# A hybrid decoder layer on one core: attention values computed with channels on partitions

## The chip, the cores and the metric

The kernel runs on one core of one Trainium2 chip. A core has TensorE (PE in the profile: matrix products and transposes, results into PSUM), VectorE (DVE), ScalarE (ACT), GpSimd (POOL) and a queue (SP) that issues the loads and stores. Each engine works through its own list in order; the engines meet through semaphores. The metric is device time in microseconds; lower is better.

## The reference, cut to what matters

One layer normalises `x` (256 rows, 1024 channels), projects it to 3840 columns, runs three branches on pieces of the projection, gates each branch with a SiLU, joins them and projects back. The change touches the attention branch (8 heads of 64 channels) and the normalisation inside the convolution branch:

```
l_own = where(dist >= 0, q @ k.T * scale - slopes * dist, NEG)   # per head, 256 x 256
p     = softmax(l_own, axis=-1)
y_m   = merge_heads(p @ v) * silu(m_gate)
...
yn    = (conv - mean) * rsqrt(var + eps) * ln_g + ln_b           # over the 256 conv channels
y_a   = (silu(yn) @ pw_w + pw_b) * silu(a_gate)
```

With 256 rows there is one attention block, so no block selection takes place.

## The kernel before, in words

Every large product is done in split form: each weight and each activation is held as a high part and a low remainder (`hi`/`lo` for weights, `xh`/`xl` for the input), and three products of a special 32-bit type are added. ACT makes the high part (line 113), DVE or POOL the low one (line 119). Products of plain float32 (scores, values, transposes) run beside them.

The projection is cut into steps, `STEPS`, in a fixed order. A step of kind `slot` makes 128 output channels with channels on partitions: 16 products with `hi`, then whatever is planned for the step's middle, then 8 with `lo`. A step of kind `row` makes a quarter of a sum over input channels for 512 output channels, with sequence rows on partitions: 8 products of 512 columns, the middle, 4 more. The tables `mid` and `then` (lines 481 to 513) say which piece of the branches stands in the middle of a step and which behind it. The order is thus written by hand: steps `mv0` to `mv3` (values), `mg0` to `mg3` (attention gate), then `mq0, mk0, mq1, mk1, ...` for four pairs of heads, then the output projection in passes `o0` to `o3` (each with a middle) and the rest of it.

For each pair of heads `hp`: `scores` multiplies queries and keys into two PSUM banks `p_sc`, one head each; DVE adds the bias and takes the extreme (442), ACT takes the exponential into `pr` and its sum into `sm` (444). `turn` transposes `pr` on PE into `p_pt` and copies it out to `pt` (454). `values` multiplies `pt` with `mv` into `p_o` with rows on partitions (465, 467); DVE divides by the sum (469) and multiplies by the gate (471). `back` transposes that to channels on partitions (476), and `put_y` splits it for the output projection (302, 303).

The convolution's taps run on DVE as a chain of 62 operations (328), spread over the steps by `FILL`. `conv_norm` transposes the result and takes its statistics; `conv_back` scales it (351), transposes it back (355) and applies the SiLU; `conv_point` is the small matrix product after that.

PSUM gives eight banks: six in a rotating pool (`bank`) and two at the side. A tile that takes over a bank waits until the last reader of the earlier one is done.

Of the kernel before, what the change touches and what calls it, by code (L numbers as in the profile page):

```python
# [35 lines left out]
A_VAL, A_GLU, A_GATE, R_Q, R_K, R_V, R_GATE, M_Q, M_K, M_V, M_GATE = (  # L36
    0, 256, 512, 768, 1024, 1280, 1536, 1792, 2304, 2816, 3328)
# [2 lines left out]

STEPS = ["rq0", "rk0", "rq1", "rk1", "ag0", "ag1"] + [f"mv{i}" for i in range(4)] + \
    [f"mg{i}" for i in range(4)] + ["mq0", "pw"] + [f"{a}{i}" for i in range(4) for a in ("mq", "mk")][1:]
SLOT = {"rq": R_Q, "rk": R_K, "ag": A_GATE, "mq": M_Q, "mk": M_K}
ROW = {"mv": M_V, "mg": M_GATE}
CH = 32

FILL = {"rq0": 4, "rk0": 5, "rq1": 4, "rk1": 4, "ag0": 4, "ag1": 5, "mv0": 5, "mv1": 5, "mv2": 5, "mv3": 5, "mg0": 5,
# [4 lines left out]
def hybrid(ctx: ExitStack, tc: tile.TileContext, xt, xn, wi, wo, taps, pw, fg, dec, bias, out):  # L52
    nc = tc.nc
    const = ctx.enter_context(tc.tile_pool(name="const", bufs=1))
    rawp = ctx.enter_context(tc.tile_pool(name="rawp", bufs=RAW))
    hlp = ctx.enter_context(tc.tile_pool(name="hlp", bufs=PARTS))
    work = ctx.enter_context(tc.tile_pool(name="work", bufs=2))
# [5 lines left out]
    def bank(name):  # L63
        return psum.tile([P, 512], F32, name=name, tag="ps")
# [10 lines left out]
    tiny = const.tile([P, 2], F32, name="tiny")  # L75
# [4 lines left out]
    ident = const.tile([P, P], F32, name="ident")  # L80
# [105 lines left out]
    rstd = const.tile([P, 2], F32, name="rstd")  # L186
# [63 lines left out]
    nc.scalar.copy(out=rb_sb, in_=rb[:, :SEQ])  # L250

    mv = const.tile([P, 2, 512], F32, name="mv")
    mg = const.tile([P, 2, 512], F32, name="mg")
    rv = const.tile([P, 2, 256], F32, name="rv")
    rgate = const.tile([P, 2, 256], F32, name="rgate")

# [37 lines left out]
    def scaled(dst, p):  # L294
        nc.vector.tensor_tensor(out=dst, in0=p, in1=rb_sb, op=ALU.mult)
# [50 lines left out]

    norms = []

    def conv_back():
        for b, p, mvv, rs in norms:  # L350
            nc.vector.tensor_scalar(yn[:, b], p[:, :256], mvv[:, 0:1], rs, op0=ALU.subtract, op1=ALU.mult)
        for c in range(2):
            p = bank(f"p_z{c}")[:, :SEQ]
            for b in range(2):
                nc.tensor.transpose(p[:, b * P:(b + 1) * P], yn[:, b, c * P:(c + 1) * P], ident)
            nc.scalar.activation(sh[:, c], p, AF.Silu, bias=lnb[c], scale=lng[c])
            nc.scalar.activation(p, p, AF.Silu, bias=lnb[c], scale=lng[c])
            nc.vector.tensor_tensor(out=sll[:, c], in0=p, in1=sh[:, c].bitcast(F32), op=ALU.subtract)
# [12 lines left out]
    rq, rk, st = {}, {}, {}  # L371

    def heads(p, name):

        t = work.tile([P, SEQ], F32, name=name, tag=name)
        scaled(t, p)
        return t
# [47 lines left out]
            put_y(2 + c, p)  # L425


    mq, mk, pt, pr, sms, po = {}, {}, {}, {}, {}, {}

    def scores(hp):  # L430
        ps = [bank(f"p_sc{hp}{a}") for a in range(2)]
        for lhs, n, o in ((slice(P, 256), 256, 0), (slice(0, P), P, 256)):
            for a in range(2):
                r = slice(HD * a, HD * (a + 1))
                nc.tensor.matmul(ps[a][:, o:o + n], mq[hp][r, lhs], mk[hp][r, :n], start=True, stop=True)  # L435
        sms[hp] = work.tile([P, 2, 2], F32, name="sm", tag="sm")
        for a in range(2):
            h = 2 * hp + a
            pr[h] = work.tile([P, 384], F32, name="pr", tag="st", bufs=4)
            mn = work.tile([P, 2], F32, name="mn", tag="mn", bufs=4)  # L440
            for b, s in ((1, slice(0, 256)), (0, slice(256, 384))):
                nc.vector.tensor_tensor_reduce(ps[a][:, s], ps[a][:, s], bias_sb[h // 4][:, h % 4, s], -0.125, 3.0e38,  # L442
                                               ALU.add, ALU.min, mn[:, b:b + 1])
                nc.scalar.activation(pr[h][:, s], ps[a][:, s], AF.Exp, bias=mn[:, b:b + 1], scale=-1.0,  # L444
                                     accum_out=sms[hp][:, b, a:a + 1])

    def turn(hp):
        for a in range(2):
            h = 2 * hp + a
            p = bank(f"p_pt{h}")  # L450
            for o, s in ((0, 256), (P, 0), (256, P)):
                nc.tensor.transpose(p[:, o:o + P], pr[h][:, s:s + P], ident)
            pt[h] = work.tile([P, 384], F32, name="pt", tag="pt", bufs=3)
            (nc.scalar.copy if a else nc.vector.tensor_copy)(out=pt[h], in_=p[:, :384])
        ri = work.tile([P, 2, 2], F32, name="ri", tag="ri")
        nc.vector.reciprocal(ri, sms[hp])
        sms[hp] = ri

    def values(hp):
        p = bank(f"p_o{hp}")[:, :SEQ].rearrange("p (b c) -> p b c", c=P)  # L460
        for b in range(2):
            for a in range(2):
                h = 2 * hp + a
                hs, d = slice(h * HD, (h + 1) * HD), slice(a * HD, (a + 1) * HD)
                nc.tensor.matmul(p[:, b, d], pt[h][:, b * P:(b + 1) * P], mv[:, 0, hs], start=True, stop=(b == 0))  # L465
                if b:
                    nc.tensor.matmul(p[:, b, d], pt[h][:, 256:], mv[:, 1, hs], start=False, stop=True)
        p4 = p.rearrange("p b (a d) -> p b a d", d=HD)
        nc.vector.tensor_tensor(out=p4, in0=p4, in1=sms[hp][:, :, :, None].to_broadcast([P, 2, 2, HD]), op=ALU.mult)
        po[hp] = work.tile([P, 2, P], F32, name="po", tag="po")  # L470
        nc.vector.tensor_tensor(out=po[hp], in0=p, in1=mg[:, :, hp * P:(hp + 1) * P], op=ALU.mult)

    def back(hp):
        p = bank(f"p_y{hp}")[:, :SEQ]
        for b in range(2):
            nc.tensor.transpose(p[:, b * P:(b + 1) * P], po[hp][:, b], ident)
        put_y(4 + hp, p)


# [1 line left out]
    first, mid, then = {}, {}, {}  # L481

    def plan(table, name, f, *args):
        table.setdefault(name, []).append(lambda: f(*args))

    def after(name, n):

        order = [s for s in STEPS if s != "pw"] + [f"o{k}" for k in range(4)]
        return order[order.index(name) + n]
# [2 lines left out]
        plan(mid, after(f"rk{c}", 1), ret_scores, c)  # L492
    plan(mid, "mv0", ret_values)
    plan(then, "mv2", ret_back)
    plan(mid, "mg3", conv_norm)
    plan(mid, "mq0", conv_back)
    plan(then, "mq0", lambda: nc.scalar.activation(tiny[:, 1:2], tiny[:, 0:1], AF.Exp))
    plan(mid, "mk1", conv_point)
    for hp in range(4):
        k = f"mk{hp}"  # L500
        plan(mid, after(k, 1), scores, hp)
        late = hp == 3
        plan(mid if late else then, after(k, 3 if late else 2), turn, hp)
# [11 lines left out]
    for name in STEPS:  # L515
        g, i = name[:2], name[-1]
        ahead(at_step[name])
        for f in first.get(name, ()):
            f()
        between = mid.get(name, ())  # L520
        if g == "pw":
            for f in between:
                f()
        elif g in ROW:
            ps = row(name, between)
            if i == "3":
                for b in range(2):
                    if g == "mv":
                        nc.scalar.activation(mv[:, b], ps[b], AF.Copy, scale=rstd[:, b:b + 1])
                    else:  # L530
                        nc.scalar.activation(mg[:, b], ps[b], AF.Silu, scale=rstd[:, b:b + 1])
# [14 lines left out]
    ps = {}  # L546
# [125 lines left out]
```

## Time and profile before

| | |
|---|---|
| median of three runs | 142.26 us (142.19 to 142.7) |
| profiled execution | 143.95 us |
| its span, first to last instruction | 142.2 us |
| mean granted TensorE clock over the span | 0.992 of full speed |
| busy share PE / POOL / DVE / ACT | 94% / 57% / 55% / 50% |
| PE from and to | 0 to 135.2 us |

The profiled execution is 1.75 us longer than its span. A row of a timeline gives start, duration, engine, line, operation, the names read and written and the shape; `x4` means that four instructions of the same kind are merged. A float32 product shows as two records and a special 32-bit one as a single record.

### The profile page before, as it was taken

What the parts mean: (1) busy time and instruction counts of PE and PEld (TensorE: products, weight loads), DVE (VectorE), ACT (ScalarE), POOL (GpSimd) and SP (SyncE); (2) the same over time, 40 slices, a digit from 0 to 9 for tenths busy, and PEclk for the clock granted to TensorE, in tenths of its full rate; (3) what the DMA queues carried; (4) which work ended last, traced back from release to release, by engine and by line L of the source; (5) the groups of instructions that cost most, each with busy time, mean ns of one, the idle gap of its engine ahead of it and who ended that gap; (6) DMA issues with size and microseconds to landing.
All of it is one profiled execution on the core that took longest, in us unless ns stands there. A gap on an engine that the chain in (4) does not pass through costs nothing.

```text
span 142.2 us, 2416 instructions
## 1 busy us (share of the span) xinstructions
PE 133.7 (94%) x884; PEld 118.9 (84%) x884; DVE 77.7 (55%) x212; ACT 71.0 (50%) x128; POOL 81.0 (57%) x51
## 2 busy tenths in 40 slices
PE   7799999999999999999999999999999999999900
PEld 2588899899999998777889999999999888988900
DVE  1446385626897799979936325544353512214460
ACT  4366489927950390059207977518357383102520
POOL 2000002596599998987994589952916639603340
PEclk9999999999999999999999999999999999999996
DMA  4999999499987887066586227667000000000124
GB/s 132 301 354 314 409 406 394 171 378 396 426 295 219 248 312 267 27 191 212 158 272 198 43 113 196 224 202 270 3 0 5 0 0 0 0 5 0 65 82 148
DMA packets 8796, 26.42 MB, mean 186 GB/s; under 512 B 1104, under 2 KB 2384, under 8 KB 8784
## 3 DMA queue, kind: packets, MB, share of 16 engines
q1 hardware_dynamic: 8496, 25.87, 53.2%
q10 hardware_dynamic: 288, 0.39, 0.8%
q8 instruction: 7, 0.11, 0.3%
q14 instruction: 5, 0.04, 0.1%
HBM read 25.21 MB, written 1.05 MB: 185 GB/s over the span
## 4 chain that ended last, share of the span: by engine, by line
PE 87%; DVE 2%; DMA 2%; POOL 2%; ACT 1%; issue 1%; POOLq 0%; DVEq 0%; SPq 0%; ACTq 0%
PE p_a L210 9%; PE p_rv L213 9%; PE p_mv L289 8%; PE p_mg L289 8%; PE p_out L195 4%; PE p_out L197 4%; PE p_out L196 4%; PE p_mq L270 3%; PE p_mk L265 3%; PE p_mk L270 3%; PE p_mq L265 3%; PE p_mq L264 3%; PE p_mk L264 3%; PE p_sc L435 2%; PE p_o L465 2%; DMA raw_g<-in_wi 2%
## 5 line engine op out<-in xcount | busy, mean ns | idle before, releaser
L119 POOL TENSOR_TENSOR lo_o<-raw_o,hi_o 128x1024 fp32r<-128x1024 f32 x8 | 18.9, 2380 | 12.7 <-ACT hi_o L113 8.5
L328 DVE SCALAR_TENSOR_TENSOR sums<-u,tp,sums 128x256 f32<-128x256 f32 x58 | 23.4, 479 | 0.0
L195 PE MATMUL p_out<-hi_o,yh 128*128 128x512 f32 (+1 forms) x40 | 14.5, 362 | 0.0
L196 PE MATMUL p_out<-hi_o,yl 128*128 128x512 f32 (+1 forms) x40 | 13.9, 349 | 0.0
L197 PE MATMUL p_out<-lo_o,yh 128*128 128x512 f32 (+1 forms) x40 | 13.9, 348 | 0.0
L183 POOL TENSOR_TENSOR rstd<-rs_t,mhalf 128x2 f32<-128x2 f32 x1 | 0.7, 720 | 22.4 <-DVE rs_t L182 22.4
L444 ACT ACTIVATE pr<-p_sc,mn 128x256 f32<-128x256 f32 (+1 forms) x16 | 6.7, 421 | 13.3 <-DVE mn L442 13.3
L113 ACT CAST hi_g<-raw_g 128x1024 fp32r<-128x1024 f32 (+1 forms) x10 | 8.8, 876 | 8.7 <-DMA raw_g<-in_wi 8.7
L119 POOL TENSOR_TENSOR lo_mq<-raw_mq,hi_mq 128x1024 fp32r<-128x1024 f32 x4 | 9.6, 2402 | 3.1 <-ACT hi_mq L113 3.1
L119 DVE TENSOR_TENSOR lo_g<-raw_g,hi_g 128x1024 fp32r<-128x1024 f32 (+1 forms) x10 | 10.0, 1006 | 1.3 <-ACT hi_g L113 1.3
L119 POOL TENSOR_TENSOR lo_mk<-raw_mk,hi_mk 128x1024 fp32r<-128x1024 f32 x4 | 9.6, 2406 | 1.0 <-ACT hi_mk L113 1.0
L119 POOL TENSOR_TENSOR lo_mg<-raw_mg,hi_mg 128x1024 fp32r<-128x1024 f32 x4 | 9.5, 2389 | 0.5 <-ACT hi_mg L113 0.5
L442 DVE CUSTOM_DVE_ANT_0 p_sc<-p_sc,bias 128x256 f32<-128x256 f32 (+1 forms) x16 | 5.7, 374 | 7.5 <-ACT pr L444 5.1
L119 POOL TENSOR_TENSOR lo_mv<-raw_mv,hi_mv 128x1024 fp32r<-128x1024 f32 x4 | 9.5, 2390 | 0.0
L197 PEld LDWEIGHTS p_out<-lo_o,yh 128*128 128x128 f32 x40 | 7.5, 188 | 1.1
L176 DVE SCALAR_TENSOR_TENSOR xl<-xt_sb,xh 128x256 fp32r<-128x256 f32 x8 | 3.9, 486 | 8.2 <-ACT xh L175 8.2
L195 PEld LDWEIGHTS p_out<-hi_o,yh 128*128 128x128 f32 x40 | 7.5, 188 | 1.0
L113 ACT CAST hi_o<-raw_o 128x1024 fp32r<-128x1024 f32 x8 | 8.3, 1048 | 0.0
L196 PEld LDWEIGHTS p_out<-hi_o,yl 128*128 128x128 f32 x40 | 7.5, 188 | 0.9
L593 POOL TENSOR_TENSOR yg<-xn_sb,fg_sb 128x512 f32<-128x512 f32 (+1 forms) x3 | 3.3, 1099 | 8.1 <-DVE xn_sb L591 8.1
L264 PE MATMUL p_mq<-xh,hi_mq 128*128 128x256 f32 x32 | 7.8, 284 | 0.0
L265 PE MATMUL p_mq<-xl,hi_mq 128*128 128x256 f32 x32 | 7.7, 279 | 0.0
(175 smaller groups left out, 385.5 us busy)
## 6 DMA issues: line engine op xcount, KB each, us to landing
raw_o<-in_wo SPq DMA_DIRECT2D x8, 512.0 KB, 4.6
raw_g<-in_wi SPq DMA_DIRECT2D x6, 512.0 KB, 7.8
raw_mv<-in_wi SPq DMA_DIRECT2D x4, 512.0 KB, 7.6
raw_mg<-in_wi SPq DMA_DIRECT2D x4, 512.0 KB, 4.9
raw_mq<-in_wi SPq DMA_DIRECT2D x4, 512.0 KB, 4.1
raw_mk<-in_wi SPq DMA_DIRECT2D x4, 512.0 KB, 4.0
bias<-in_bias SPq DMA_DIRECT2D x2, 768.0 KB, 8.5
raw_g<-in_wi SPq DMA_DIRECT2D x4, 256.0 KB, 4.2
```

The source lines that it names most:

```text
L113: nc.scalar.copy(out=hi, in_=raws[j])
L119: eng.tensor_tensor(out=lo, in0=raws.pop(j), in1=hi.bitcast(F32), op=ALU.subtract)
L195: nc.tensor.matmul(p, lh, rh, start=first, stop=False)
L196: nc.tensor.matmul(p, ll, rh, start=False, stop=False)
L197: return nc.tensor.matmul(p, lh, rl, start=False, stop=last)
L210: nc.tensor.matmul(pa[c], wt[:, c * P:(c + 1) * P], xs[:, k], **flags)
L213: nc.tensor.matmul(pv[b], xs[:, k, b * P:(b + 1) * P], wt, **flags)
L264: nc.tensor.matmul(p, hi[:, s], xh[:, k], start=(k == 0), stop=False)
L265: nc.tensor.matmul(p, hi[:, s], xl[:, k], start=False, stop=False)
L270: nc.tensor.matmul(p, lo[:, s], xh[:, k], start=False, stop=(k == KC - 1))
L289: nc.tensor.matmul(row_banks[g][b], (xl if part else xh)[:, k, b * P:(b + 1) * P], (lo if w else hi)[:, s], start=(k == 0 and w == 0 and p ...
L328: nc.vector.scalar_tensor_tensor(to[c], u[:, c, t:t + SEQ], w, sums[c], op0=ALU.mult, op1=ALU.add)
```

## The change

Attention values: `values` now holds `mv` still and streams `pt`, so that `p_o` comes out with channels on partitions: head 0 of the pair on partitions 0 to 63, head 1 on 64 to 127. `back` and its transposes go. Since the row sum can no longer be applied there, `scores` divides by it: the exponential stays in the PSUM bank `p_sc`, and DVE multiplies it by the reciprocal on the way to `pr`. The gate must have channels on partitions too, so `mg0` to `mg3` become four `slot` steps with a DVE scaling and an ACT SiLU each. `turn` and `values` of the first three pairs move half a step or a step later. `conv_norm` moves behind `mg3`, the scaling of `conv_back` becomes `conv_scale` behind `mq0`, and the rest of it stands in the middle of `mk0`.

```diff
-SLOT = {"rq": R_Q, "rk": R_K, "ag": A_GATE, "mq": M_Q, "mk": M_K}
-ROW = {"mv": M_V, "mg": M_GATE}
+SLOT = {"rq": R_Q, "rk": R_K, "ag": A_GATE, "mg": M_GATE, "mq": M_Q, "mk": M_K}
+ROW = {"mv": M_V}
...
-    def conv_back():
+    def conv_scale():
         for b, p, mvv, rs in norms:
             nc.vector.tensor_scalar(yn[:, b], p[:, :256], mvv[:, 0:1], rs, op0=ALU.subtract, op1=ALU.mult)
+
+    def conv_back():
...
-                nc.scalar.activation(pr[h][:, s], ps[a][:, s], AF.Exp, bias=mn[:, b:b + 1], scale=-1.0,
-                                     accum_out=sms[hp][:, b, a:a + 1])
+                nc.scalar.activation(ps[a][:, s], ps[a][:, s], AF.Exp, bias=mn[:, b:b + 1], scale=-1.0,
+                                     accum_out=sm[:, b:b + 1])
+            soft.append((pr[h], ps[a], sm, halves))
+        for p, e, sm, halves in soft:
+            ri = work.tile([P, 2], F32, name="ri", tag="ri", bufs=4)
+            nc.vector.reciprocal(ri, sm)
+            for b, s in halves:
+                nc.vector.tensor_scalar(p[:, s], e[:, s], ri[:, b:b + 1], None, op0=ALU.mult)
...
     def values(hp):
-        p = bank(f"p_o{hp}")[:, :SEQ].rearrange("p (b c) -> p b c", c=P)
-        for b in range(2):
+        p = bank(f"p_o{hp}")[:, :SEQ]
+        for part in range(2):
             for a in range(2):
                 h = 2 * hp + a
-                hs, d = slice(h * HD, (h + 1) * HD), slice(a * HD, (a + 1) * HD)
-                nc.tensor.matmul(p[:, b, d], pt[h][:, b * P:(b + 1) * P], mv[:, 0, hs], start=True, stop=(b == 0))
-                if b:
-                    nc.tensor.matmul(p[:, b, d], pt[h][:, 256:], mv[:, 1, hs], start=False, stop=True)
...
-    def back(hp):
...
+                hs, r = slice(h * HD, (h + 1) * HD), slice(HD * a, HD * (a + 1))
+                if part == 0:
+                    nc.tensor.matmul(p[r], mv[:, 0, hs], pt[h][:, :256], start=True, stop=False)
+                else:
+                    nc.tensor.matmul(p[r, P:], mv[:, 1, hs], pt[h][:, 256:], start=False, stop=True)
+        nc.vector.tensor_tensor(out=p, in0=p, in1=mgate[:, hp], op=ALU.mult)
         put_y(4 + hp, p)
...
-    plan(mid, "mg3", conv_norm)
-    plan(mid, "mq0", conv_back)
-    plan(then, "mq0", lambda: nc.scalar.activation(tiny[:, 1:2], tiny[:, 0:1], AF.Exp))
+    plan(then, "mg3", conv_norm)
+    plan(then, "mq0", conv_scale)
+    plan(mid, "mk0", conv_back)
+    plan(mid, "mk0", lambda: nc.scalar.activation(tiny[:, 1:2], tiny[:, 0:1], AF.Exp))
...
-        late = hp == 3
-        plan(mid if late else then, after(k, 3 if late else 2), turn, hp)
-        plan(mid, after(k, 4 if late else 3), values, hp)
-        if late:
-            plan(then, "o3", back, hp)
-        else:
-            plan(mid, after(k, 4), back, hp)
+        plan(mid, after(k, 3), turn, hp)
+        plan(mid, after(k, 4), values, hp)
...
-            if g == "ag":
-                t = agate[:, int(i)]
+            if g in ("ag", "mg"):
+                t = (agate if g == "ag" else mgate)[:, int(i)]
                 scaled(t, p)
                 nc.scalar.activation(t, t, AF.Silu)
```

PE, before: what stands from behind step `mk1` to the middle of `mk2` beside the projection's own products (`p_pt` are the transposed weights of heads 0 and 1, `p_o` their values, `p_sc` the scores of heads 2 and 3, `p_y` the transposes back).

```order
L452 MATMUL p_pt_1128<-ident,pr 128x128 x3
L452 MATMUL p_pt_1134<-ident,pr 128x128 x3
...
L465 MATMUL p_o_1165<-mv,pt 128x64 x3
L467 MATMUL p_o_1165<-mv,pt 128x64
L465 MATMUL p_o_1165<-mv,pt 128x64
L467 MATMUL p_o_1165<-mv,pt 128x64
L435 MATMUL p_sc_1175<-mk,mq 128x256
L435 MATMUL p_sc_1176<-mk,mq 128x256
L435 MATMUL p_sc_1175<-mk,mq 128x128
L435 MATMUL p_sc_1176<-mk,mq 128x128
L270 MATMUL p_mq_1148<-xh,lo_mq_987 128x256 x8
...
L476 MATMUL p_y_1227<-ident,po 128x128 x2
```

PE, now, the same stretch: `turn` and the next scores in the middle of `mq2`, the values in the middle of `mk2`.

```order
L462 MATMUL p_pt_1216<-ident,pr 128x128 x3
L462 MATMUL p_pt_1222<-ident,pr 128x128 x3
L437 MATMUL p_sc_1228<-mk,mq 128x256
L437 MATMUL p_sc_1229<-mk,mq 128x256
L437 MATMUL p_sc_1228<-mk,mq 128x128
L437 MATMUL p_sc_1229<-mk,mq 128x128
L270 MATMUL p_mq_1199<-xh,lo_mq_1030 128x256 x8
...
L473 MATMUL p_o_1289<-pt,mv 64x256 x2
L475 MATMUL p_o_1289<-pt,mv 64x128 x2
L270 MATMUL p_mk_1272<-xh,lo_mk_1036 128x256 x8
```

Six `p_o` products of 64 columns have become four, two of 256 columns and two of 128, on half the partitions each; they stand half a period later, and `p_y` is gone.

DVE, before: from the last bias step of heads 0 and 1 to the scaled keys of step `mk1`, which the next scores read, and the copy of `p_pt`.

```order
L442 ISA mn 128x1
L295 TENSOR_TENSOR mq<-p_mq_1029,rb_sb 128x256
L367 SCALAR_TENSOR_TENSOR p_pw_1098<-p_pw_1098,ch,agate 128x256
L303 TENSOR_TENSOR yl<-p_pw_1098,yh 128x256
L367 SCALAR_TENSOR_TENSOR p_pw_1108<-p_pw_1108,ch,agate 128x256
L303 TENSOR_TENSOR yl<-p_pw_1108,yh 128x256
L295 TENSOR_TENSOR mk<-p_mk_1081,rb_sb 128x256
L454 COPY pt<-p_pt_1128 128x384
L456 RECIPROCAL ri<-sm 128x4
```

DVE, now, the same place.

```order
L453 RECIPROCAL ri<-sm 128x2
L455 TENSOR_SCALAR pr<-p_sc_1102,ri 128x256
L455 TENSOR_SCALAR pr<-p_sc_1102,ri 128x128
L453 RECIPROCAL ri<-sm 128x2
L455 TENSOR_SCALAR pr<-p_sc_1103,ri 128x256
L455 TENSOR_SCALAR pr<-p_sc_1103,ri 128x128
L295 TENSOR_TENSOR mq<-p_mq_1085,rb_sb 128x256
L369 SCALAR_TENSOR_TENSOR p_pw_1163<-p_pw_1163,ch,agate 128x256
L303 TENSOR_TENSOR yl<-p_pw_1163,yh 128x256
L369 SCALAR_TENSOR_TENSOR p_pw_1173<-p_pw_1173,ch,agate 128x256
L303 TENSOR_TENSOR yl<-p_pw_1173,yh 128x256
L295 TENSOR_TENSOR mk<-p_mk_1146,rb_sb 128x256
```

Six instructions now stand ahead of the scaled queries and keys of the next pair; the single reciprocal behind the copy is gone.

## Rows read from the trace of the kernel before

**Rows 1.** Page, parts 1 and 4: busy time of each engine; the ending chain by engine.

```profile
PE 133.7 (94%) x884; PEld 118.9 (84%) x884; DVE 77.7 (55%) x212; ACT 71.0 (50%) x128; POOL 81.0 (57%) x51
...
PE 87%; DVE 2%; DMA 2%; POOL 2%; ACT 1%; issue 1%; POOLq 0%; DVEq 0%; SPq 0%; ACTq 0%
```

**Rows 2.** Waits of PE: who it waited for, total us, times, longest.

```profile
PE p_warm L73 <- PEq L664: 0.8, 1, 0.8
PE p_a L210 <- ACT hi_g L113: 0.7, 1, 0.7
```

**Rows 3.** Timeline of PE, 78 to 94 us: start, duration, what.

```profile
78.67 0.28 PE L264 MATMUL p_mk<-xh,hi_mk 128*128 128x256 f32 x1
...
81.47 0.28 PE L264 MATMUL p_mq<-xh,hi_mq 128*128 128x256 f32 x1
...
85.33 0.28 PE L264 MATMUL p_mk<-xh,hi_mk 128*128 128x256 f32 x1
...
89.56 0.82 PE L452 MATMUL p_pt<-ident,pr 128*128 128x128 f32 x6
...
92.08 0.78 PE L465 MATMUL p_o<-mv,pt 128*128 128x64 f32 x6
...
93.46 0.92 PE L435 MATMUL p_sc<-mk,mq 64*128 64x256 f32 x8
```

**Rows 4.** Timeline of PE, 120 to 125 us, pair 3: values, then transposes back.

```profile
120.89 0.78 PE L465 MATMUL p_o<-mv,pt 128*128 128x64 f32 x6
...
122.14 0.48 PE L195 MATMUL p_out<-hi_o,yh 128*128 128x512 f32 x1
122.46 0.39 PE L196 MATMUL p_out<-hi_o,yl 128*128 128x512 f32 x1
...
123.63 0.38 PE L476 MATMUL p_y<-ident,po 128*128 128x128 f32 x2
123.76 0.48 PE L195 MATMUL p_out<-hi_o,yh 128*128 128x512 f32 x1
124.08 0.39 PE L196 MATMUL p_out<-hi_o,yl 128*128 128x512 f32 x1
```

**Rows 5.** Timeline of PE, windows inside the scores of pair 0.

```profile
83.43 0.49 PE L435 MATMUL p_sc<-mk,mq 64*128 64x256 f32 x2
...
83.75 0.38 PE L435 MATMUL p_sc<-mk,mq 64*128 64x256 f32 x2
...
83.97 0.39 PE L435 MATMUL p_sc<-mk,mq 64*128 64x128 f32 x4
```

**Rows 6.** Timeline of DVE, 84 to 92 us: pair 0 after its scores.

```profile
84.38 0.43 DVE L442 CUSTOM_DVE_ANT_0 p_sc<-p_sc,bias 128x256 f32<-128x256 f32 x1 [2.29 <-PE p_sc L435]
...
85.51 0.30 DVE L442 CUSTOM_DVE_ANT_0 p_sc<-p_sc,bias 128x128 f32<-128x128 f32 x1 [0.63 <-ACT pr L444]
...
87.10 0.42 DVE L295 TENSOR_TENSOR mq<-p_mq,rb_sb 128x256 f32<-128x256 f32 x1
88.11 0.49 DVE L367 SCALAR_TENSOR_TENSOR p_pw<-p_pw,ch,agate 128x256 f32<-128x256 f32 x1 [0.60 <-PE p_pw L197]
...
90.65 0.41 DVE L295 TENSOR_TENSOR mk<-p_mk,rb_sb 128x256 f32<-128x256 f32 x1
```

**Rows 7.** Groups of DVE by form: count, busy us, mean ns, idle before.

```profile
L351 DVE TENSOR_SCALAR yn<-p_ln,ln_mv,ln_r 128x256 f32<-128x256 f32 x2 | 1.1, 543 | 0.2 <-POOL ln_r L183 0.2
...
L456 DVE RECIPROCAL ri<-sm 128x4 f32<-128x4 f32 x4 | 0.7, 168 | 0.0
```

**Rows 8.** Timeline of PE, 71 to 78 us: last gate step, transposes back of the convolution.

```profile
72.19 0.63 PE L289 MATMUL p_mg<-hi_mg,xh 128*128 128x512 f32 x2
...
75.42 0.28 PE L264 MATMUL p_mq<-xh,hi_mq 128*128 128x256 f32 x1
...
77.30 0.60 PE L355 MATMUL p_z<-ident,yn 128*128 128x128 f32 x4
```

**Rows 9.** Timeline of DVE, 60 to 81 us: taps, and scaled queries of pair 0.

```profile
62.04 9.49 DVE L328 SCALAR_TENSOR_TENSOR sums<-u,tp,sums 128x256 f32<-128x256 f32 x24
...
79.99 0.41 DVE L295 TENSOR_TENSOR mq<-p_mq,rb_sb 128x256 f32<-128x256 f32 x1
```

More of the change, by code (lines that the diff above doesn't have):

```diff
@@ L252, in hybrid @@
     mv = const.tile([P, 2, 512], F32, name="mv")
-    mg = const.tile([P, 2, 512], F32, name="mg")
+    mgate = const.tile([P, 4, SEQ], F32, name="mgate")
     rv = const.tile([P, 2, 256], F32, name="rv")
@@ L425, in ret_back @@
             put_y(2 + c, p)
-    mq, mk, pt, pr, sms, po = {}, {}, {}, {}, {}, {}
+    mq, mk, pt, pr = {}, {}, {}, {}
     def scores(hp):
@@ L435, in scores @@
                 nc.tensor.matmul(ps[a][:, o:o + n], mq[hp][r, lhs], mk[hp][r, :n], start=True, stop=True)
-        sms[hp] = work.tile([P, 2, 2], F32, name="sm", tag="sm")
+        soft = []
         for a in range(2):
@@ L440, in scores @@
             mn = work.tile([P, 2], F32, name="mn", tag="mn", bufs=4)
-            for b, s in ((1, slice(0, 256)), (0, slice(256, 384))):
+            sm = work.tile([P, 2], F32, name="sm", tag="sm", bufs=4)
+            halves = ((1, slice(0, 256)), (0, slice(256, 384)))
+            for b, s in halves:
                 nc.vector.tensor_tensor_reduce(ps[a][:, s], ps[a][:, s], bias_sb[h // 4][:, h % 4, s], -0.125, 3.0e38,
                                                ALU.add, ALU.min, mn[:, b:b + 1])
-                nc.scalar.activation(pr[h][:, s], ps[a][:, s], AF.Exp, bias=mn[:, b:b + 1], scale=-1.0,
-                                     accum_out=sms[hp][:, b, a:a + 1])
+                nc.scalar.activation(ps[a][:, s], ps[a][:, s], AF.Exp, bias=mn[:, b:b + 1], scale=-1.0,
[4 more added lines that the diff above has]
+            nc.vector.reciprocal(ri, sm)
+            for b, s in halves:
+                nc.vector.tensor_scalar(p[:, s], e[:, s], ri[:, b:b + 1], None, op0=ALU.mult)
     def turn(hp):
@@ L454, in turn @@
             (nc.scalar.copy if a else nc.vector.tensor_copy)(out=pt[h], in_=p[:, :384])
-        ri = work.tile([P, 2, 2], F32, name="ri", tag="ri")
-        nc.vector.reciprocal(ri, sms[hp])
-        sms[hp] = ri
     def values(hp):
-        p = bank(f"p_o{hp}")[:, :SEQ].rearrange("p (b c) -> p b c", c=P)
-        for b in range(2):
+        p = bank(f"p_o{hp}")[:, :SEQ]
+        for part in range(2):
             for a in range(2):
                 h = 2 * hp + a
-                hs, d = slice(h * HD, (h + 1) * HD), slice(a * HD, (a + 1) * HD)
-                nc.tensor.matmul(p[:, b, d], pt[h][:, b * P:(b + 1) * P], mv[:, 0, hs], start=True, stop=(b == 0))
-                if b:
-                    nc.tensor.matmul(p[:, b, d], pt[h][:, 256:], mv[:, 1, hs], start=False, stop=True)
[L468 to L471, printed above, removed]
-    def back(hp):
-        p = bank(f"p_y{hp}")[:, :SEQ]
-        for b in range(2):
-            nc.tensor.transpose(p[:, b * P:(b + 1) * P], po[hp][:, b], ident)
+                hs, r = slice(h * HD, (h + 1) * HD), slice(HD * a, HD * (a + 1))
[4 more added lines that the diff above has]
+        nc.vector.tensor_tensor(out=p, in0=p, in1=mgate[:, hp], op=ALU.mult)
         put_y(4 + hp, p)
@@ L527, in hybrid @@
                 for b in range(2):
[L528 to L531, printed above, removed]
+                    nc.scalar.activation(mv[:, b], ps[b], AF.Copy, scale=rstd[:, b:b + 1])
         else:
             p = slot(name, between)
-            if g == "ag":
-                t = agate[:, int(i)]
+            if g in ("ag", "mg"):
+                t = (agate if g == "ag" else mgate)[:, int(i)]
                 scaled(t, p)
```

## The prediction

> **What bounds the kernel now.** I read the page first: PE is busy 94% of the span and carries 87% of the chain that ended last [rows 1]. Then PE's own waits: two, 1.5 us together, both at the start [rows 2]. From there to its last product PE never waits, so every microsecond of PE's list is a microsecond of the kernel, and the other engines matter only where a change makes PE wait for them. What follows PE's last product (the final norm and the stores) is not touched. So I priced PE's list from its timeline [rows 3 to 5], and then asked, with DVE's timeline, whether the new DVE work comes in time [rows 6, 7, 9].
>
> **Prices on PE.** A step with nothing in its middle takes 81.47 - 78.67 = 2.80 us for 24 products of 256 columns, 0.117 each [rows 3]; one of 512 columns counts as two, 0.233. The next step, with scores in its middle, takes 85.33 - 81.47 = 3.86: scores cost 1.06, of which 0.09 is lost before they start (16 products would end at 83.34, they start at 83.43) [rows 3, 5].
>
> **Values and transposes back, removed.** Values alone run from 120.89 to 122.14, 1.25 us, and the first product behind them holds PE 0.32 instead of 0.23: 1.34 [rows 4]. With scores behind them (pairs 0 to 2) it is 93.46 - 92.08 - 0.09 = 1.29 [rows 3]. The two transposes back: 0.13, and again 0.09 behind them: 0.22 [rows 4]. Together 3 x 1.29 + 1.34 + 4 x 0.22 = 6.09 us off PE's list. These values were short (64 columns) and paid a weight load for each record: twelve records in 1.34 us.
>
> **Values, added.** Four products a pair, two of 256 columns and two of 128, each on half of the array's columns. The trace has none such. The nearest row is the scores: the same column counts, each on half of the array's rows. There the two heads run at once: two records start together at 83.43, two at 83.75, and four short ones from 83.97 [rows 5]. A pair of 256-column records thus takes 83.97 - 83.75 = 0.22, a pair of 128 half of it; running time 2 x 0.22 + 2 x 0.11 = 0.66 of the 1.06, the rest is the first load and the change of array shape. Bounds per pair: if the shape change costs no more than 0.09 at each end, 0.84; if the halves run one after the other, another 0.66, so 1.72. I take 1.06, the row of the scores: 4 x 1.06 = 4.24.
>
> The Trainium skill, "TensorE: Matmul & The Clock Gate", section Part 3 (packing small matmuls), gives 2.38 times for three column tiles of 32; at the same efficiency two tiles would run 1.59 times as fast as one, an estimate of 0.83 instead of 0.66, and the sum below would become -0.9. No row before shows a column tile, so the sum stays with the scores.
>
> **Gate as slots.** A gate step before is 75.42 - 72.19 = 3.23, less the four transposes of `conv_norm` in its middle. A slot is 2.80 and 24 x 0.117 equals 12 x 0.233, so PE pays nothing for the exchange (and the transposes are 0.43) [rows 3, 8]. DVE gains four scalings (0.42 each, as the queries in [rows 6]), ACT four SiLUs for two longer ones. The cast of `mk0`'s weights now stands on ACT behind the second gate's SiLU, that is behind the end of `mg1` (72.19 - 2.80 = 69.39); `mk0` starts at 78.67, so 9 us cover it and POOL's low part behind it. SP's loads keep their order.
>
> What isn't hidden: the taps. DVE did 24 of them in 9.49 us, 0.395 each, with no gap [rows 9]. Now the scaling of `mg2` stands ahead of the last six and waits for PE: last product of `mg2` ends at 72.19 - 0.12 + 0.28 = 72.35, scaling to 72.8, six taps to 75.1. The transposes in `conv_norm`, now behind `mg3`, want the result at 72.19 + 2.80 = 74.99, the second channel half 0.1 later. Wait: about 0.1, ends 0 and 0.4 (if DVE answers PE late each time).
>
> **Convolution norm in two steps.** The same instructions, and they land on another pair of queries and keys. Before, from `p_z` at 77.30 to the end of the scaled `mq0` 3.10 us pass (79.99 + 0.41) [rows 8, 9]; now the scaled `mk0` stands at that place on DVE, and the scores read it. PE fills the time from the transposes to the scores with 0.43 + 8 x 0.117 + 16 x 0.117 = 3.23. Cover 0.1: cost 0; without cover the difference goes to PE, up to 0.3.
>
> **Softmax divided on DVE.** Per pair: two reciprocals (0.17, [rows 7]), two scalings of 256 and two of 128 from PSUM. A 256 one lies between 0.42 (queries [rows 6]) and 0.54 (line 351, the same operation with two scalars [rows 7]); a 128 one is 0.13 shorter, as the bias steps show (0.43 against 0.30, [rows 6]). So 1.76 to 2.24 a pair; I take 0.45 and 0.30, 1.84 in all. The exponential keeps its length on ACT, only its target changes. What is queued behind these six on DVE: the scaled queries and keys of the next pair, and PE needs the keys for the next scores. With T the start of pair 0's scores (83.43): queries at T + 3.67 (87.10) before; now + 5.51. From there 0.41 to the first `p_pw` operation (88.11 less its wait of 0.60) and 90.65 - 88.11 + 0.41 = 2.95 to the end of the keys [rows 6]: T + 8.87. PE comes to the scores of pair 1 at T + 6.13 (start of the transposes before, 89.56) + 1.87 (half of `mq2`) + 0.65 (transposes, now there) + 0.09 = T + 8.74 [rows 3]. Wait 0.13, with the hand-over 0.15; ends 0 and 0.55. Pair 2: keys ready at about 3.67 + 1.84 + 0.41 + half of 2.54 + 0.41 = 7.6 after pair 1's scores, PE there at 0.97 + 0.93 + 1.87 + 1.06 + 0.93 + 1.87 + 0.65 + 0.09 = 8.4: cover 0.8. Pair 3: six products of 512 columns stand there instead of 16 of 256, 1.40 for 1.87, so 7.9: cover 0.3. Banks: `mq2` takes over head 0's scores and waits for their division, T + 3.67 + 0.92 = T + 4.6, where PE comes at T + 6.13. The transposes themselves have 2.5 us. With fewer DVE steps behind the last values and five microseconds of other products, pair 3's end costs nothing.
>
> **Sum.** -6.09 + 4.24 + 0.10 + 0.15 = -1.60 us. On the profiled execution: 143.95 - 1.60 = 142.35. Without the profiler the runs' median is 142.26, so I predict 142.26 - 1.60 = 140.65 us. The forecast's own range: values at 0.84 and no waits, -2.73; values 1.06 and waits 0.4 + 0.55, -0.90; so 139.5 to 141.35.
>
> **Rivals.**
> *The halves run one after the other* (slower). Place: the four values blocks. 1.72 each, 6.88: -6.09 + 6.88 + 0.25 = +1.04, 143.3 us. It breaks even at (6.09 - 0.25) / 4 = 1.46 a block and is slower by over 0.5% from 1.64. For it: no row shows column halves at work, and both heads' weights lie across all rows. Against it: row halves do run together [rows 5], and the two halves here read and write apart. Chance 0.10.
>
> *The loads come out from behind the products* (no change). Between 83.43 and 83.75 lie 0.32 where a record pair takes 0.22: one load shows, 0.10 [rows 5]. If each of a block's four record pairs showed its load, the block would take 1.06 + 0.30 = 1.36 and the sum -0.40, 141.86 us. Against it: in an ordinary step a load of every product is hidden at 0.117 a product, on the same rows of the array [rows 3]. Chance 0.10. The Trainium skill speaks for this one: the same page and section says that a weight load overlaps a running product only where the row groups differ, and column halves share theirs. By that rule the block costs what this rival says; the trace before does not agree for whole-array products, and is silent on halves.
>
> *DVE becomes late for every pair.* Price: what the division takes over 1.84 goes to PE at each of three scores once the covers (0, 0.8, 0.3) are used. At 2.84 a pair: 1.15 + 0.2 + 0.7 = 2.05 of waits, sum +0.3, 142.55 us. For it: DVE's queue is strict and the keys stand last. Against it: no row of that size on DVE is over 0.54. Chance 0.05.
>
> **How the numbers follow.** Forecast 0.72, the three rivals 0.25, and 0.03 for something unseen, half of it slower. Below 0.5% (0.7 us) this kernel's measurement cannot be told from no change: the forecast lies beyond that on the faster side nearly whole (0.71), the second and third rivals within it. Faster 0.72, same 0.16, slower 0.12. Range: from 139.7, leaving the forecast's last corner out, up to 142.6, which takes in the second and third rivals and leaves out the first.
>
> **What would show it.** Right: in the profile after, pairs of `p_o` records on 64 partitions start within 0.01 us of each other, a values block lengthens its step by about 1.0 to 1.1; no `p_y`; PE's waits grow by two small ones, for the last taps and for `mk` of pair 1. Wrong: `p_o` records of one head starting only when the other's end (first rival); 0.3 between the starts of all record pairs (second); waits of PE on `mk` over 0.5 us (third). The forecast also fails if PE shows a wait that I have not listed, in the gate steps above all, where DVE and PE now answer each other three times.

## Result, and the profile after

The changed kernel takes 140.51 us (median of four runs, 139.92 to 140.92) against 142.36 for the kernel before on the same chip: ratio 0.985, 95% interval 0.980 to 0.990. The forecast was 140.65 us. Two single executions further down are left out of the ratios: 164.97 us of the changed kernel at a granted clock of 0.758, and 259.79 us of the kernel with the division twice.

The two profiled spans lie 3.4 us apart (142.2 and 138.8), more than the medians. The surplus lies at the start: the first product of the gate comes at 63.79 us before and at 62.34 after, and nothing of the change stands ahead of it. It moves by itself: in two experiments below that leave this front as it was, it came at 62.06 and at 63.52. So I compare kernels by a second measure that leaves the start out: the time from the start of PE's first gate product (`p_mg`) to the start of its last product, read from each timeline. That is 134.93 - 63.79 = 71.14 us before and 131.58 - 62.34 = 69.24 after: -1.90 us, where the medians say -1.85. It is one trace for each kernel, so how well it repeats was not measured as a whole; blocks that no edit touches agree to 0.01 us (the scores of pair 0 take 0.85 us up to the next product in all twelve traces).

The page after, busy time of each engine and the ending chain; it answers to [rows 1]:

```profile
PE 130.6 (94%) x908; PEld 115.0 (83%) x908; DVE 83.6 (60%) x232; ACT 71.9 (52%) x130; POOL 81.0 (58%) x51
...
PE 64%; DMA 17%; ACT 5%; DVE 5%; SPq 2%; POOL 2%; issue 2%; POOLq 0%; DVEq 0%; ACTq 0%
```

DVE does 5.9 us more, PE 3.1 us less. PE's share of the chain falls from 87% to 64% because of the start alone: the chain now runs through the first loads and what hangs on them up to 36.55 us, ahead of the stage that was changed, and from there to 125.57 us it is PE and nothing else. Who PE waited for (total us, times, longest), answering to [rows 2]:

```profile
PE p_warm L73 <- PEq L657: 0.8, 1, 0.8
PE p_a L210 <- ACT hi_g L113: 0.2, 1, 0.2
```

Nothing new that the list would show: PE is the bound of the changed stage as before, and the gain is what left its list. The new values block of pair 0, timeline of PE (start, duration, line, what), with some windows narrowed so that records come apart; it answers to [rows 3, 4]:

```profile
92.84 0.28 PE L264 MATMUL p_mk<-xh,hi_mk 128*128 128x256 f32 x1
...
94.81 0.44 PE L473 MATMUL p_o<-pt,mv 128*64 128x256 f32 x2
...
95.08 0.39 PE L473 MATMUL p_o<-pt,mv 128*64 128x256 f32 x2
95.29 0.28 PE L475 MATMUL p_o<-pt,mv 128*64 128x128 f32 x2
...
95.61 1.21 PE L270 MATMUL p_mk<-xh,lo_mk 128*128 128x256 f32 x8
...
96.66 0.28 PE L264 MATMUL p_mq<-xh,hi_mq 128*128 128x256 f32 x1
```

The step takes 96.66 - 92.84 = 3.82 us where an empty one takes 2.80: the block costs 1.02, and the three others 0.99 to 1.00 by the same count. `x2` at one start is the sight to look for: both heads' records start together (94.81, 95.08, 95.29), so the two column halves of the array work at once. The step from pair to pair is 0.27, then 0.21. From 94.81 to 95.61 are 0.80 us; about 0.1 is lost ahead of the first record, and 0.1 in the products behind the block.

The division on DVE after the scores of pair 0, which start at 82.16 (timeline of DVE; answers to [rows 6]):

```profile
85.89 0.16 DVE L453 RECIPROCAL ri<-sm 128x2 f32<-128x2 f32 x1
86.09 0.74 DVE L455 TENSOR_SCALAR pr<-p_sc,ri 128x256 f32<-128x256 f32 x2
...
87.60 0.41 DVE L295 TENSOR_TENSOR mq<-p_mq,rb_sb 128x256 f32<-128x256 f32 x1
...
90.46 0.41 DVE L295 TENSOR_TENSOR mk<-p_mk,rb_sb 128x256 f32<-128x256 f32 x1
```

And PE at the scores of pair 1:

```profile
90.15 0.82 PE L462 MATMUL p_pt<-ident,pr 128*128 128x128 f32 x6
90.93 0.92 PE L437 MATMUL p_sc<-mk,mq 64*128 64x256 f32 x8
```

From the first reciprocal to the scaled queries 1.71 us pass. The keys end at 90.87; PE's scores of pair 1 start at 90.93, 0.78 behind the transposes at 90.15 where the two pairs behind it take 0.75.

### The profile page after: what moved, and what is told of

It is laid out like the page before. It is cut to its first block, busy times and chain, and to the rows that moved or that the text cites. A ratio compares the mean times of both kernels' runs of the same rounds, so it can differ in the third digit from the quotient of the medians.

```text
span 138.8 us, 2481 instructions
## 1 busy us (share of the span) xinstructions
PE 130.6 (94%) x908; PEld 115.0 (83%) x908; DVE 83.6 (60%) x232; ACT 71.9 (52%) x130; POOL 81.0 (58%) x51
## 4 chain that ended last, share of the span: by engine, by line
PE 64%; DMA 17%; ACT 5%; DVE 5%; SPq 2%; POOL 2%; issue 2%; POOLq 0%; DVEq 0%; ACTq 0%
PE p_mv L289 8%; DMA raw_rk<-in_wi 7%; DMA xn_sb<-in_xn 6%; PE p_out L195 4%; DMA raw_g<-in_wi 4%; PE p_out L197 4%; PE p_out L196 4%; PE p_mq L270 3%; PE p_mk L270 3%; PE p_mk L265 3%; PE p_mg L264 3%; PE p_mq L265 3%; PE p_mq L264 3%; PE p_mg L270 3%; PE p_mg L265 3%; PE p_mk L264 3%
## 5 line engine op out<-in xcount | busy, mean ns | idle before, releaser
L448 ACT ACTIVATE p_sc<-p_sc,mn 128x256 f32<-128x256 f32 (+1 forms) x16 | 6.3, 395 | 6.2 <-DVE mn L446 4.4
L264 PE MATMUL p_mk<-xh,hi_mk 128*128 128x256 f32 x32 | 7.7, 279 | 0.0
```

What stands on the lines that cost most here:

```text
L264: nc.tensor.matmul(p, hi[:, s], xh[:, k], start=(k == 0), stop=False)
L448: nc.scalar.activation(ps[a][:, s], ps[a][:, s], AF.Exp, bias=mn[:, b:b + 1], scale=-1.0, accum_out=sm[:, b:b + 1])
```

## Experiments

"Gate to end" is the measure above, from one trace of each kernel; the median and the ratio are of all its executions. Ratios are to the kernel before, run beside each: its own median went from 142.22 to 142.68, so ratios can be compared and medians only roughly.

| kernel | median, us | ratio (95%) | gate to end, us | against the changed kernel |
|---|---|---|---|---|
| before | 142.36 | | 71.14 | +1.90 |
| changed | 140.51 | 0.985 (0.980 to 0.990) | 69.24 | |
| both heads on one half | 143.20 | 1.006 (1.002 to 1.010) | 71.88 | +2.64 |
| head after head | 140.53 | 0.985 (0.980 to 0.989) | 69.28 | +0.04 |
| values twice | 142.77 | 1.003 (1.000 to 1.006) | 71.93 | +2.69 |
| division twice | 142.94 | 1.003 (1.000 to 1.007) | 71.77 | +2.53 |
| old places | 142.63 | 0.999 (0.997 to 1.002) | 71.19 | +1.95 |
| taps moved | 140.27 | 0.985 (0.982 to 0.989) | 69.06 | -0.18 |
| old places and taps | 142.42 | 1.000 (0.998 to 1.002) | 71.05 | +1.81 |
| before + division | 143.69 | 1.011 (1.009 to 1.012) | 72.41 | +3.17 |
| before + division, moved | 142.93 | 1.005 (1.002 to 1.008) | 71.61 | +2.37 |
| before + conv norm moved | 142.09 | 1.001 (0.998 to 1.003) | 71.10 | +1.86 |

The changed kernel itself, run once more beside the variants of places and taps, took 140.70 (ratio 0.986, 0.984 to 0.988):

> The changed kernel once more, beside the three variants of it, as the base they are compared with: 140.5 us, 1.8 us under the kernel before.

### Both heads on one half of the columns

```diff
-        for part in range(2):
-            for a in range(2):
...
-                hs, r = slice(h * HD, (h + 1) * HD), slice(HD * a, HD * (a + 1))
...
-                    nc.tensor.matmul(p[r], mv[:, 0, hs], pt[h][:, :256], ...)
...
+        for a in range(2):
+            for part in range(2):
...
+                hs, o = slice(h * HD, (h + 1) * HD), SEQ * a
...
+                    nc.tensor.matmul(w[:HD, o:o + SEQ], mv[:, 0, hs], pt[h][:, :256], ...)
...
+        nc.vector.tensor_copy(out=p[HD:], in_=w[:HD, SEQ:2 * SEQ])
```

> The changed kernel, but both heads' values go through the same half of the array's columns (partitions 0 to 63 of PSUM, the second head beside the first in the bank), head after head, and a copy on DVE moves the second head to partitions 64 to 127 ahead of the gate. My theory, that the change gains because the two halves of the columns run at once: the running time of a block doubles from 0.66 to 1.32 us, a block takes 1.66 instead of the 1.0 seen after the change, 4 x 0.66 = 2.6 us more than the changed kernel, about 143.1 us, the price of the forecast's first rival: slower than before. Rival (a block's time is its weight loads and its change of array shape, not the columns that stream): less than 0.8 us more, under 141.4 us. The DVE copies cost nothing: the queue has covers of 0.3 us and more there.

Timeline of PE, pair 0:

```profile
94.84 0.65 PE L474 MATMUL p_o<-pt,mv 128*64 128x256 f32 x2
95.32 0.38 PE L476 MATMUL p_o<-pt,mv 128*64 128x128 f32 x2
95.54 0.59 PE L474 MATMUL p_o<-pt,mv 128*64 128x256 f32 x2
95.97 0.38 PE L476 MATMUL p_o<-pt,mv 128*64 128x128 f32 x2
96.28 1.21 PE L270 MATMUL p_mk<-xh,lo_mk 128*128 128x256 f32 x8
```

The same eight records now come in two rounds, and the block lasts 96.28 - 94.84 = 1.44 instead of 0.80. The surplus, 0.64 a block and 2.64 in all, is the first rival's price to 0.02 a block, and it makes the kernel 0.6% slower than before. So it is the working at once of the two halves on which the sign of this change rests.

### Head after head

```diff
-        for part in range(2):
-            for a in range(2):
+        for a in range(2):
+            for part in range(2):
```

> The changed kernel with the four products of a values block in the other order: both products of the first head, then both of the second, each still on its own half of the columns. Theory A, PE starts products in program order and a product waits only for its own half: the second head's long product (0.44 us) starts with the first head's short one (0.22), so a block runs 0.44 + 0.44 + 0.22 = 1.10 instead of 0.66, 4 x 0.44 = +1.8 us, 142.3 us. Theory B, each half has a queue of its own: no difference, 140.5 us. Theory C, only neighbours of the same shape run at once: no overlap, +2.6 us, 143.1 us.

Timeline of PE, pair 0:

```profile
94.74 0.44 PE L473 MATMUL p_o<-pt,mv 128*64 128x256 f32 x2
...
95.22 0.28 PE L475 MATMUL p_o<-pt,mv 128*64 128x128 f32 x2
95.55 1.21 PE L270 MATMUL p_mk<-xh,lo_mk 128*128 128x256 f32 x8
```

Theory B holds; A and C fall. The second head's long product stands third in the program, behind the first head's short one, and yet it starts with the first head's long one (`x2` at 94.74; two records of one product would start 0.27 apart), 0.48 us before the product ahead of it in the program (95.22). The block lasts 0.81. It looks as if each half took the next product meant for it, as theory B has it; this is also where PE does not keep to one list in order. The Trainium skill, "TensorE: Matmul & The Clock Gate", section Part 3, says that products start and end strictly in program order, with no reordering. Across column halves this run differs, and the measurement decides.

### Values twice

```diff
-        for part in range(2):
+        for part in (0, 1, 0, 1):
```

> The changed kernel with every values block issued twice (same result, the first pass is overwritten). It splits the 1.0 us of a block into running time and what is paid once. Theory: 0.66 us of running time per block and 0.34 paid once for the first load and the change of array shape, so +0.66 each, 4 x 0.66 = +2.6 us, about 143.1 us. Rival (the loads of the halves are not hidden and everything scales): +1.0 each, +4.0 us, about 144.5 us. With halves one after the other it would be +1.3 each, +5.3 us, 145.8 us.

Timeline of PE, pair 0:

```profile
94.43 0.65 PE L473 MATMUL p_o<-pt,mv 128*64 128x256 f32 x4
94.91 0.39 PE L475 MATMUL p_o<-pt,mv 128*64 128x128 f32 x4
95.13 0.60 PE L473 MATMUL p_o<-pt,mv 128*64 128x256 f32 x4
95.56 0.39 PE L475 MATMUL p_o<-pt,mv 128*64 128x128 f32 x4
95.88 1.21 PE L270 MATMUL p_mk<-xh,lo_mk 128*128 128x256 f32 x8
```

1.45 against 0.80: the second round of eight records costs 0.65. That this is running time alone shows in its parts: the two long record pairs take 95.56 - 95.13 = 0.43 and the two short ones of the first round, with half the columns, 95.13 - 94.91 = 0.22, half as much, so that nothing is left over for a load to each. Eight more loads show nothing, and the second rival (each load comes out, 0.3 a block) falls. The rule that spoke for it (the same page and section of the Trainium skill: a load overlaps only where row groups differ) is not borne out: both halves use all rows, and their loads are hidden. What is left of a block, about 0.36, is paid once.

### Division twice

```diff
-            for b, s in halves:
-                nc.vector.tensor_scalar(p[:, s], e[:, s], ri[:, b:b + 1], None, op0=ALU.mult)
+            for _ in range(2):
+                for b, s in halves:
+                    nc.vector.tensor_scalar(p[:, s], e[:, s], ri[:, b:b + 1], None, op0=ALU.mult)
```

> The changed kernel with the four scalings of the softmax division done twice per pair (same result): about 1.65 us more on DVE per pair, nothing more on PE or ACT. Theory (third rival's price: pair 1's keys are just in time, covers of 0.8 and 0.3 us for pairs 2 and 3): PE waits 1.65 at the scores of pair 1, 0.85 at pair 2 and 1.35 at pair 3, +3.5 to +3.9 us, about 144.2 us, slower than before. Rival (DVE has slack enough behind the scores, its share of busy time is only 60%): no difference, 140.5 us.

Waits of PE (total us, times, longest):

```profile
PE p_sc L437 <- DVE mk L295: 2.3, 3, 1.3
```

Timeline of PE at the scores of pair 1:

```profile
90.09 0.82 PE L463 MATMUL p_pt<-ident,pr 128*128 128x128 f32 x6
92.17 0.92 PE L437 MATMUL p_sc<-mk,mq 64*128 64x256 f32 x8 [1.26 <-DVE mk L295]
```

Place and mechanism are those of the third rival: the scores wait for the scaled keys behind the division on DVE, three times. The size was too high, since a scaling behind another one adds less than its own duration: from reciprocal to queries 85.83 to 88.84, 3.01 us instead of 1.71, so 1.30 more and not 1.65. From transposes to scores PE then took 2.08, 1.10 and 1.56 us where the changed kernel takes 0.78, 0.75 and 0.75: 1.30, 0.36 and 0.81 lost, 2.47 in all. The covers of pairs 2 and 3 are thus 0.94 and 0.49 (forecast 0.8 and 0.3), that of pair 1 nothing.

### Transposes and values at their old places, and the taps

```diff
-        plan(mid, after(k, 3), turn, hp)
-        plan(mid, after(k, 4), values, hp)
+        late = hp == 3
+        plan(mid if late else then, after(k, 3 if late else 2), turn, hp)
+        plan(mid, after(k, 4 if late else 3), values, hp)
```

> The changed kernel with the transposes and the values of pairs 0 to 2 back at the places they had before: transposes behind the keys' step, values straight ahead of the next pair's scores, so that the two blocks that split the array stand side by side. Theory (about 0.35 us of each values block is paid for changing the array's shape and the first load): a block between whole-array products pays it twice, side by side once; -0.1 to -0.2 for each of three pairs and the 0.05 of pair 1's wait gone, -0.35 to -0.65 us. Rival (the transposes come too early for the division on DVE, or the scores wait for a bank): PE waits on pr or p_sc, 0 to +1.0 us.

Waits of PE, then its timeline at pair 0's values and the transposes of pairs 1 and 2:

```profile
PE p_pt L462 <- DVE pr L455: 1.3, 4, 0.4
PE p_o L473 <- DVE pt L464: 0.4, 1, 0.4
```

```profile
91.17 0.65 PE L473 MATMUL p_o<-pt,mv 128*64 128x256 f32 x4 [0.41 <-DVE pt L464]
...
91.97 0.92 PE L437 MATMUL p_sc<-mk,mq 64*128 64x256 f32 x8
92.83 1.21 PE L270 MATMUL p_mq<-xh,lo_mq 128*128 128x256 f32 x8
93.87 0.28 PE L264 MATMUL p_mk<-xh,hi_mk 128*128 128x256 f32 x1
...
97.15 0.55 PE L462 MATMUL p_pt<-ident,pr 128*128 128x128 f32 x3 [0.32 <-DVE pr L455]
98.09 0.52 PE L462 MATMUL p_pt<-ident,pr 128*128 128x128 f32 x3 [0.40 <-DVE pr L455]
...
106.25 0.55 PE L462 MATMUL p_pt<-ident,pr 128*128 128x128 f32 x3 [0.17 <-DVE pr L455]
107.19 0.52 PE L462 MATMUL p_pt<-ident,pr 128*128 128x128 f32 x3 [0.39 <-DVE pr L455]
```

The time is the opposite of my theory's, and the rival was too mild. The whole gain is gone: the divided probabilities come late for the transposes of pairs 1 and 2 (0.32 and 0.40, then 0.17 and 0.39), and in pair 0 the copy `pt` on DVE stands behind the convolution's point product and the scaled keys, so that the values wait 0.41.

The prize for neighbours is there all the same, under these waits. From start to start the two blocks take 0.80 and 0.86 (91.17, 91.97, 92.83), as each does alone; but what a block loses outside of that, 0.1 ahead of its first record and 0.1 in the products behind it, is now lost once for both. From the first values to the next step are 93.87 - 91.17 = 2.70 us, or 1.77 without the eight products of 0.117. Alone, the values take 96.66 - 94.81 - 0.93 = 0.92 by that count (rows of the result) and the scores 85.33 - 83.43 - 0.93 = 0.97 [rows 3, 5], together 1.89, and the scores another 0.09 ahead of their start. So neighbours save about 0.2 a pair, 0.6 in all, the upper end of my theory (pair 1 shows the same 2.70, and pair 2 is taken to save as much); the waits then come to an estimated 1.95 + 0.6 = 2.55 us, of which PE's list shows 1.7.

The Trainium skill, "TensorEngine Tiling (Array Packing)", section Tiling Modes, says that a change of tiling mode drains the engine. Column halves to row halves is such a change, and these rows are in line with it: neither block gets shorter from its start to the next one's start. None of them shows a drain as such.

The taps, on the changed kernel:

```diff
-FILL = {..., "mv3": 5, "mg0": 5, "mg1": 5, "mg2": 6}
+FILL = {..., "mv3": 7, "mg0": 6, "mg1": 6, "mg2": 2}
```

> The changed kernel with the 24 taps handed out otherwise over the steps (7 behind mv3, 6 behind mg0, 6 behind mg1, 2 behind mg2 instead of 5, 5, 5, 6), so that two rather than six taps stand behind the scaling of mg2. Theory (PE waits 0.18 us for the last taps at the conv norm's transposes in the changed kernel): the transposes' step falls from 0.61 to 0.43, -0.18 us. Rival (the 0.18 us is the cost of the transposes between slots, not of the taps): 0. Either lies under what the whole time can tell, so the profile decides: the time from the first gate product to the last one of PE.

The last two taps on DVE, then PE at the convolution's transposes, in the changed kernel:

```profile
72.85 0.86 DVE L328 SCALAR_TENSOR_TENSOR acc<-u,tp,sums 128x256 f32<-128x256 f32 x2
```

```profile
73.55 0.77 PE L338 MATMUL p_ln<-ident,acc 128*128 128x128 f32 x4
74.08 0.37 PE L264 MATMUL p_mq<-xh,hi_mq 128*128 128x256 f32 x1
```

The same with the taps moved:

```profile
70.90 0.86 DVE L328 SCALAR_TENSOR_TENSOR acc<-u,tp,sums 128x256 f32<-128x256 f32 x2
```

```profile
73.16 0.60 PE L338 MATMUL p_ln<-ident,acc 128*128 128x128 f32 x4
73.51 0.36 PE L264 MATMUL p_mq<-xh,hi_mq 128*128 128x256 f32 x1
```

0.53 falls to 0.35: the wait for the last taps, which ended at 73.71 in the changed kernel and now at 71.76, was 0.18 and is gone. PE's list of waits shows it in neither kernel, only the longer group does. The whole time (140.27) is not to be told from the changed kernel's; the trace puts this version 0.18 us ahead, the fastest of all.

> Both edits together, the taps handed out otherwise and the transposes and values of pairs 0 to 2 at their places of before. They touch different stages, so the theory has them add up: -0.5 to -0.8 us against the changed kernel, about 139.9 us. Rival: only the taps' 0.18, 140.3 us.

Against the old places alone 71.05 - 71.19 = -0.14: the taps' part adds up; the waits at the old places are the same as without it.

### The division alone, at the old places and at the new

The kernel before, with the division on DVE as in the change and nothing else; then `turn` and `values` placed as in the change, `back` a step later.

```diff
-                nc.scalar.activation(pr[h][:, s], ps[a][:, s], AF.Exp, ...)
+                nc.scalar.activation(ps[a][:, s], ps[a][:, s], AF.Exp, ...)
...
+            nc.vector.reciprocal(ri, sm)
+            for b, s in halves:
+                nc.vector.tensor_scalar(p[:, s], e[:, s], ri[:, b:b + 1], None, op0=ALU.mult)
...
-        nc.vector.tensor_tensor(out=p4, in0=p4, in1=sms[hp][:, :, :, None].to_broadcast([P, 2, 2, HD]), op=ALU.mult)
```

> The kernel before with one part of the change alone: the softmax divided on DVE ahead of the transposes; values, transposes back, gate, conv norm and all places as before. Theory A, from the run with the transposes and values at their places of before: the divided probabilities come about 0.65 us too late for the transposes of pairs 1 and 2, and the copy of pair 0's transposes stands too late on DVE for its values (0.5), so PE waits 1.8 us and the kernel takes about 144.1 us, slower. Theory B, the division is hidden on DVE wherever the transposes stand: 142.3 us, no difference.

Timeline of PE:

```profile
90.87 0.66 PE L470 MATMUL p_o<-mv,pt 128*128 128x64 f32 x4 [0.34 <-DVE pt L462]
...
97.30 1.11 PE L460 MATMUL p_pt<-ident,pr 128*128 128x128 f32 x6
98.16 0.37 PE L264 MATMUL p_mq<-xh,hi_mq 128*128 128x256 f32 x1
```

The first bias step of pair 1 on DVE, here, and then with the new values at the old places:

```profile
93.31 0.43 DVE L444 CUSTOM_DVE_ANT_0 p_sc<-p_sc,bias 128x256 f32<-128x256 f32 x1 [0.42 <-PE p_sc L435]
```

```profile
93.44 0.43 DVE L446 CUSTOM_DVE_ANT_0 p_sc<-p_sc,bias 128x256 f32<-128x256 f32 x1
```

Slower, by theory A's mechanism: pair 0's values lose 0.5 against the kernel before, the scores behind them 0.1 more, and the six transposes of pair 1 take 0.86 up to the next product instead of 0.57 (pair 2 0.89), 0.3 each and not 0.65. In all +1.27 where 1.8 was expected. With the new values at the old places PE waits about twice as long by the estimate above, mostly because their result is split by DVE (`put_y`) ahead of the next bias step: that step begins 1.47 us behind the start of pair 1's scores (93.44 - 91.97) and here 0.96 (93.31 - 92.35), so that the division comes half a microsecond earlier.

> As the last one (the kernel before with the division alone), but with the transposes and values of pairs 0 to 2 at the places that the change gives them, each a step or half a step later, and the transposes back a step later too. Theory A (the move is what makes room for the division): the waits fall to under 0.2 us, 142.3 us, as before; what the change then gains comes all from the values' other form. Theory B (the moved places cost something of their own, or the division waits for a bank): over 0.7 us more than before.

Timeline of PE at the scores of pair 3, then of DVE:

```profile
109.19 1.25 PE L435 MATMUL p_sc<-mk,mq 64*128 64x256 f32 x8
110.37 0.50 PE L195 MATMUL p_out<-hi_o,yh 128*128 128x512 f32 x1
```

```profile
109.04 0.42 DVE L303 TENSOR_TENSOR yl<-p_y,yh 128x256 fp32r<-128x256 f32 x1 [1.59 <-ACT yh L302]
```

No wait for the division is left, and the waits on `pt` and `pr` are gone, as theory A has it; but +0.47 remain, by theory B. Most of it is one place: scores that take 0.85 elsewhere take 1.18 up to the next product. The second head's bank is held by pair 1's transposes back until DVE has read it (109.04 + 0.42 = 109.46). That `p_y`, which I moved, is not in the changed kernel at all. Some 0.14 are left for the rest of the move, spread thin.

### The conv norm's places alone

```diff
...
-    plan(mid, "mg3", conv_norm)
-    plan(mid, "mq0", conv_back)
...
+    plan(then, "mg3", conv_norm)
+    plan(then, "mq0", conv_scale)
+    plan(mid, "mk0", conv_back)
...
```

> The kernel before with the conv norm's new places alone: its transposes behind mg3, its scaling behind mq0, the transposes back in the middle of mk0; the gate as before, so no scaling of mg2 stands ahead of the last taps. Theory: PE pays nothing, 142.3 us, and the step at the transposes costs the 0.43 us of before, since the taps end earlier than they are wanted. Rival (the 0.18 us seen there in the changed kernel, and something at the first scores, come from the new places themselves): +0.2 to +0.4 us at these two places.

Timeline of PE:

```profile
73.41 0.60 PE L338 MATMUL p_ln<-ident,acc 128*128 128x128 f32 x4
73.77 0.36 PE L264 MATMUL p_mq<-xh,hi_mq 128*128 128x256 f32 x1
```

0.36 at the transposes and -0.04 over the whole stage: the places cost nothing, and the 0.18 of the changed kernel belongs to the `mg2` scaling ahead of the taps. The run also settles the gate, since it still has the row form: from the first gate product to these transposes 73.41 - 62.22 = 11.19 us, and 73.55 - 62.34 = 11.21 with four slots.

## Why the prediction was right, point by point

The forecast lies 0.14 us from the median, closer than its sum deserves. Values, taps, keys and conv norm missed by -0.24, +0.08, -0.12 and -0.04, together -0.32 on -1.60; the kernel before, measured again, came out 0.1 higher (142.36 for 142.26), which took part of that back by chance.

- **What bounds it.** PE's list did: a stage of which 1.9 us of list went became 1.9 us shorter, with no wait over 0.2 us put in its place.
- **Removed, 6.09.** Taken from rows of the kernel before; no run takes out these products alone. It stands as far as the rest of the sum closes: -6.09 + 4 x 1.00 (values) + 0.18 (taps) + 0.03 (keys) - 0.04 (conv norm) = -1.92, measured -1.90.
- **Values added, 4 x 1.06.** Measured 0.99 to 1.02. Taking the row halves of the scores as the model for column halves was right: running time 0.65 by the doubled block (forecast 0.66), and the first records come 0.27 apart instead of 0.32. That 0.05 a block is most of the main miss, 0.24 us in all.
- **The estimate of 0.83** running time for two column tiles, worked out from a figure of the Trainium skill ("TensorE: Matmul & The Clock Gate", section Part 3), was too high: they ran twice as fast as one (0.65 against the 1.29 that 0.65 + 0.64 of both heads on one half make).
- **Taps, 0.10.** 0.18, inside its ends; the mechanism shown by moving the taps.
- **Keys of pair 1, 0.15.** About 0.03 (0.78 against 0.75 in pairs 2 and 3). The division took 1.71 us of DVE's list against 1.84, because each scaling starts before the one ahead has ended; so the durations added up (1.97) overstate it. That pair 1 has no cover, and pairs 2 and 3 about 0.9 and 0.5, the doubled division showed.
- **Gate as slots, conv norm: nothing.** Shown by the run with the conv norm alone.
- **First rival**: a real price (2.64 us) for a thing that didn't happen. **Second**: refuted by the doubled values. **Third**: its mechanism is real, and its covers were near right (0.9 and 0.5 for 0.8 and 0.3); but the division came out 0.13 shorter than forecast, not 1.0 longer.
- **What I had not priced.** The move of `turn` and `values` by half a step or a step. I took it as given and asked only whether the division is in time where it now stands. The old places cost 1.95 us with the new values and the division alone 1.27 with the old. Beside the division, the new form takes off 1.22 at the old places (72.41 to 71.19) and 2.37 at the new ones (71.61 to 69.24, of which 0.33 is the bank held by the moved `p_y`), so the move is about as large a part of the gain as the form. The move without the division was not run.

## What to carry to other kernels

When a bound engine's list gets shorter because work moves to another engine, the gain stands or falls with the place at which the result is wanted: look through the helper's queue for what stands behind the added work, and move the consumer until the result is there first (covers of 0 to 0.9 us were enough here). Two heads of 64 channels run at once if each has its own half of the array: here by rows in the scores and by columns in the values. A chain of overlapping instructions is priced from the first start to the next one's start, not from the sum of durations; and where the start of a program varies, compare the stage that the change touches, not the span.

## What the runs showed that I had not expected

- A column half starts its own next product ahead of an earlier one of the other half: 0.48 us ahead in the run head after head.
- Small stalls hide from the list of waits: 0.18 us (taps), 0.33 us (a bank inside the scores) and 0.3 us (transposes of pair 1 with the division alone) all stood only in a group that lasted longer than its twin.
- A values block between whole-array products pays about 0.36 us over its running time, about 0.1 of it at each end. Beside the scores, which split the array by rows, one end is paid once for both: about 0.2 a pair, which the waits for the division ate up at the old places.
